# The score products of an HGRN2 scan: four products of 128 columns, or one of 128 and four of 64

## The chip, the cores and the metric

The kernel runs on one core of one Trainium2 chip. The metric is the device time of one launch in microseconds (us). The time before is 2856.59 us, the median of 3 runs that lie between 2854.42 and 2858.09 us. The profile is of one further execution on the same core.

The engines are named as the profile names them: PE (TensorE, the matrix unit; its weight loads have a row of their own, PEld), DVE (VectorE), ACT (ScalarE), POOL (GpSimd) and SP (which only issues DMAs here). L550 means line 550 of the kernel. A "product" is below one call of the matrix multiply in the kernel's source; in float32 each such call becomes two load-and-multiply pairs on PE.

## What is computed

One layer of a hybrid trunk on 2048 latent tokens of width 1024 with a prefix of 256 context tokens: RMS norm, a bidirectional HGRN2 recurrence with 8 heads of width 128, a gated readout, and a convolutional FFN of width 2816. What matters here is the recurrence in its chunkwise form, for one head and one direction:

```python
b = jnp.cumsum(logf, axis=3)                 # decay since the chunk's start
qe = q * jnp.exp(b - b_ref)
ke = k * jnp.exp(b_ref - b)
scores = jnp.einsum('bhnik,bhnjk->bhnij', qe, ke)
scores = jnp.where(mask, scores, 0.0)        # causal
o_intra = jnp.einsum('bhnij,bhnjv->bhniv', scores, v)
```

Backward in time the same is done with the order of tokens reversed, and the outputs of the two directions are added. The reference point `b_ref` of a pair of tokens may be any point as long as both factors stay in range; the result does not depend on it.

## The kernel before

**Stages.** The first 80 us load inputs and make the modulation rows. From there to about 1330 us runs the scan (`mixer_scan`), then a second pass of the scan with the readout, the output projection and the FFN. Only the scan is touched.

**Loops of the scan.** The 18 tiles of 128 tokens (2 of context, 16 of latents) form 6 units of 3 tiles, in two groups of three units (`GROUPS`). For each group, each of 8 heads and each unit of the group, `unit` is called: 48 calls, 3 tiles each. Of the 144 tiles, 16 are context tiles, which get no scores; 128 get them. A tile is split into 4 segments of 32 tokens; a unit has 12 (`NS`).

**One unit.** PE multiplies the normalized input with the head's weights (L356 to L358, three products in a reduced float32 for each part, into `z`), and ACT and DVE turn them into forget gates `F`, values `v`, the gate `st` and queries `q`. DVE scans `F` to running products `S` inside each segment (L448, L461). Then come, for both directions and all 12 segments at once, `ke` (keys, L453 and L454), `rt` (the reciprocal of a segment's whole decay, L463) and `qp` (queries with the decay up to a segment's edge, L467 and L468). POOL makes small tables of segment decays (`TB`, `TX`), and the helper `scaled` (its DVE instruction is L492) multiplies segments by them: `kd`, `qe`, `qi`, `qm`, `km`. In `qe` each query is multiplied by the reciprocal decay of its own segment. ACT copies half of the segments of `ke` to `kx` (L517, L518).

**Scores of a tile** (`part_a`). PE transposes `kd` (L542) and makes four products of 128 by 128 into one PSUM tile `sc`:

- `ke` with `qe` of direction 0 (L550; backward in time) and of direction 1 (L551; forward), of which only the four diagonal blocks of 32 by 32 are used;
- `kx` with a mix of `qp` of both directions (L556), of which the blocks between the two segments of a 64-token pair are used;
- `km` with `qm` (L557), of which the blocks between the two pairs are used.

ACT copies the two quarters of the last to `af` (L561, L562); DVE puts the others there and in `ab` under masks (`copy_predicated`, L563 with `mx`, L564 with `mb`, L565 with `mf`) and adds the two to `at` (L566). In `part_b` PE multiplies `kt` and `v` (L574, the update of the state), `qi` and the state `Sf` (L589) and `at` and `v` (L590); DVE updates `Sf` (L593).

**Order.** The `part_a` and `part_b` calls of a unit are not run in that unit. They are handed on as a list `todo`, and the next unit runs them between its own products (`fill`), in the order part_a 0, part_a 1, part_b 0, part_a 2, part_b 1, part_b 2. So the operands of a score product are made about a unit ahead of it, save in the last unit. On each engine the instructions stand in the order in which they were emitted, with small shifts that the framework makes. Tiles such as `ke`, `qp`, `qe`, `kx` have two buffers, which two units take in turn.

Of the kernel before, what the change touches and what calls it, by code (L numbers as in the profile page):

```python
# [9 lines left out]
F32 = mybir.dt.float32  # L10
F32R = mybir.dt.float32r
BF16 = mybir.dt.bfloat16
U32 = mybir.dt.uint32
AF = mybir.ActivationFunctionType
OP = mybir.AluOpType
# [29 lines left out]
NS = 12  # L45
# [3 lines left out]
def body(ctx, tc, a, out):  # L49
    nc = tc.nc  # L50
    pe, act, dve, pool, sp = nc.tensor, nc.scalar, nc.vector, nc.gpsimd, nc.sync
# [38 lines left out]
    def pool_(stack, name, bufs=1, **kw):  # L90
        return stack.enter_context(tc.tile_pool(name=name, bufs=bufs, reuse_waits="tile", **kw))
# [94 lines left out]
    with ExitStack() as c0:  # L186
# [15 lines left out]
        first = [t for u in GROUPS[0] for t in u]  # L202
        for k in range(KT):
            for i in range(2):
# [3 lines left out]
                for n in range(2):  # L208
                    pe.matmul(mps[2 * i + n], silv[:, k, :], wt[:, n * 512:(n + 1) * 512],
                              start=k == 0, stop=k == KT - 1)  # L210
# [16 lines left out]
        for g in range(2):  # L227
            ks = slice(g * 4, g * 4 + 4)
            for j, hm in enumerate(hms):
                m = 0 if first[j] >= 0 else 1  # L230
# [9 lines left out]
        mx = p0.tile([128, 16], F32, name="mx")  # L240
# [38 lines left out]
    def mixer_scan():  # L279
        gp = pool_(c1, "gp", side="right")  # L280
        xp = pool_(c1, "xp", side="right")
        ps = pool_(c1, "ps", space=PSUM)
# [3 lines left out]
        def in_block(m, blk):  # L286
            n = 128 // blk
            pool.affine_select(out=m, in_=m, pattern=[[-blk, n], [0, blk]],
                               compare_op=OP.is_ge, fill=0.0, base=0, channel_multiplier=1)
            pool.affine_select(out=m, in_=m, pattern=[[blk, n], [0, blk]],  # L290
                               compare_op=OP.is_ge, fill=0.0, base=blk - 1, channel_multiplier=-1)

        def mask(name):
            m = fix.tile([128, 4, 32], F32, name=name)
            pool.memset(m, 1.0)
            return m

        mf, mb, mx = mask("mf"), mask("mb"), mask("mx")
        in_block(mb, 32)
        in_block(mx.rearrange("p (a c) b -> p a (c b)", c=2), 64)  # L300
        dve.tensor_tensor(mx, mx, mb, OP.subtract)
        in_block(mf, 32)
        for m, s in ((mf, 1), (mb, -1)):

            pool.affine_select(out=m, in_=m, pattern=[[32 * s, 4], [s, 32]],
                               compare_op=OP.is_ge, fill=0.0, base=0, channel_multiplier=-s)
        mfu, mbu, mxu = [m.rearrange("p a b -> p (a b)").bitcast(U32) for m in (mf, mb, mx)]
        d1 = fix.tile([128, NS, SEG], BF16, name="d1")
        pool.memset(d1, 0.0)
        pool.memset(d1[:, :, 0:1], 1.0)  # L310
# [51 lines left out]
        def unit(h, w, u, tiles, todo, fine=False):  # L362
# [5 lines left out]
            g0 = 4 * s0  # L368
            lat = slice(g0, NS)
# [82 lines left out]
            ke = gp.tile([128, 2, NS, 32], F32, name="ke", tag="ke", bufs=2)  # L452
# [9 lines left out]
            rt = gp.tile([128, 2, NS], F32, name="rt", tag="rt", bufs=2)  # L462
            dve.reciprocal(rt[:, :, lat], S[:, :, lat, 32])  # L463

            qp = gp.tile([128, 2, NS, 32], F32, name="qp", tag="qp", bufs=2)
# [23 lines left out]
            def scaled(dst, src, w):  # L489

                w = w[..., None].to_broadcast(list(w.shape) + [32])
                dve.tensor_tensor(dst, src, w, OP.mult)  # L492
# [7 lines left out]
            scaled(kd, ke, TBf[:, 0:4:3])  # L500


            qe = gp.tile([128, 2, NS, 32], F32, name="qe", tag="qe", bufs=2)
            scaled(qe[:, :, lat], qp[:, :, lat], rt[:, :, lat])
            qi = gp.tile([128, 2, NS, 32], F32, name="qi", tag="qi", bufs=2)
            scaled(qi[:, :, lat], qp[:, :, lat], TBf[:, 1:3, lat])

# [1 line left out]
            qm = gp.tile([128, NSC, 4, 32], F32, name="qm", tag="qm", bufs=2)  # L509
            km = gp.tile([128, NSC, 4, 32], F32, name="km", tag="km", bufs=2)  # L510
# [2 lines left out]
            scaled(km[:, s0:, 0:2], seg(ke[:, 1])[:, :, 0:2], TX[:, 1, s0:, 0:2])  # L513
            scaled(km[:, s0:, 2:4], seg(ke[:, 0])[:, :, 2:4], TX[:, 1, s0:, 2:4])

            kx = gp.tile([128, NS, 32], F32, name="kx", tag="kx", bufs=2)
            act.activation(kx[:, g0::2], ke[:, 1, g0::2], AF.Copy)  # L517
            act.activation(kx[:, g0 + 1::2], ke[:, 0, g0 + 1::2], AF.Copy)  # L518

            if s0:  # L520
                z = ps.tile([128, s0, 128], F32, name="z", tag="pj", bufs=3)
# [16 lines left out]
            def part_a(s):  # L538
                g4 = slice(4 * s, 4 * s + 4)
                tr = ps.tile([128, 2, 128], F32, name="tr", tag="tr")  # L540
                for d in range(2):
                    pe.transpose(tr[:, d], kd[:, d, g4], ident)  # L542
                kt = gp.tile([128, 2, 128], F32, name="kt", tag="kt", bufs=3)
                act.activation(kt, tr, AF.Copy)
                kts[s] = kt
                if s < s0:
                    return

                sc = ps.tile([128, 4, 128], F32, name="sc", tag="sc", bufs=2)
                pe.matmul(sc[:, 0], ke[:, 0, g4], qe[:, 0, g4], start=True, stop=True)  # L550
                pe.matmul(sc[:, 1], ke[:, 1, g4], qe[:, 1, g4], start=True, stop=True)  # L551

                c0 = qp[:, 0, 4 * s]
                qx = bass.AP(tensor=c0.tensor, offset=c0.offset,
                             ap=[list(c0.ap[0]), [64, 2], [(NS + 1) * 32, 2], [1, 32]])
                pe.matmul(sc[:, 2], kx[:, g4], qx, start=True, stop=True)  # L556
                pe.matmul(sc[:, 3], km[:, s], qm[:, s], start=True, stop=True)  # L557
                at = gp.tile([128, 128], F32, name="at", tag="at", bufs=2)
                af, ab = ABs[count["A"] % 2]
                count["A"] += 1  # L560
                act.activation(af[0:64, 64:128], sc[0:64, 3, 64:128], AF.Copy)  # L561
                act.activation(af[64:128, 0:64], sc[64:128, 3, 0:64], AF.Copy)  # L562
                dve.copy_predicated(af, mxu, sc[:, 2])  # L563
                dve.copy_predicated(af, mbu, sc[:, 0])  # L564
                dve.copy_predicated(ab, mfu, sc[:, 1])  # L565
                dve.tensor_tensor(at, af, ab, OP.add)  # L566
                ats[s] = at

            def part_b(s):
# [33 lines left out]
                sp.dma_start(stash[t][:, 0, h, 1], qi[:, 0, g4].rearrange("p g t -> p (g t)"))  # L603

            order = ((part_a, 0), (part_a, 1), (part_b, 0), (part_a, 2), (part_b, 1), (part_b, 2))
            return [lambda f=f, s=s: f(s) for f, s in order]

# [47 lines left out]
        for g, units in enumerate(GROUPS):  # L655
            for h in range(NH):
                if g == h == 0:
                    w = head0
                else:
                    w = load_feat(h)  # L660
                    load_vg(h, w)
                for u, tiles in enumerate(units):
                    todo, fine = list(unit(h, w, u, tiles, todo, fine)), False
                    if h > 0 and steps < 16 * (g + 1):
                        next(rest, None)
                        steps += 1
                    if g == h == u == 0:
                        todo, fine = with_h(todo, [m[-2:] for m in third], [None] * 3), True
                        todo = [m[0] for m in third[1:]] + todo
                    if g == 0 and h == NH - 2 and u == 2:  # L670
                        todo += [m[0] for m in new[0:2]]
                    if g == 0 and h == NH - 1:
                        loads = [m[0] for m in new[3 * u + 2:3 * u + 5]]
                        todo = with_h(todo, [m[1:] for m in new[3 * u:3 * u + 3]],
                                      loads + [None] * (3 - len(loads)))
                        fine = True
                    if g == 1 and h == NH - 1:
                        if u == 0:
                            todo.append(gate1)
                        for j, k in enumerate(range(3 * u, min(3 * u + 3, KT))):  # L680
                            todo.insert(len(todo) if u < 2 else j,
                                        lambda k=k: out_weight(k))
        for f in todo:
            f()

    mixer_scan()
    c1.close()

# [63 lines left out]
    qp = pool_(fq, "qp", side="right")  # L752
# [70 lines left out]
    first = [Pair(1, q) for q in range(2)]  # L823
# [225 lines left out]
    ps = pool_(fp, "psa", 2, space=PSUM)  # L1049
# [200 lines left out]
    ps = pool_(fb, "psb", 8, space=PSUM)  # L1250
# [169 lines left out]
    for s in range(N):  # L1420
        ph, c = divmod(s, NC)
# [84 lines left out]
```

## Time and profile before

| what | us |
|---|---|
| median of 3 runs | 2856.59 |
| span of the profiled execution, first to last instruction | 2852.8 |
| median less span | 3.8 |
| PE busy in the span | 2803.9 |
| DVE busy in the span | 2080.8 |
| ACT busy in the span | 1176.5 |

The page gives the profiled execution by its span; the 3.8 us between it and the median of the runs lie ahead of the first and behind the last instruction, so the profiled execution's own time is taken as that median. Busy time of an engine is the union of its instructions; PE's instructions are pipelined and overlap, so the start of one to the start of the next, not its duration, is what it costs. The timeline gives starts in us from the start of the span and joins neighbours of one group ("x2": two instructions, the duration from the first one's start to the last one's end). The view of one tile gives shortest, median and longest duration in ns, and the first and last start in us.

### The profile page before, as it was taken

The numbers are of one execution on the slowest core, as the hardware profiler recorded it, in microseconds if no ns is written. First come the engines' busy times: TensorE is split into PE (matmuls) and PEld (weight loads), VectorE is DVE, ScalarE is ACT, GpSimd is POOL, SyncE is SP. The second block draws the span as 40 slices with busy tenths as digits, with TensorE's granted clock in tenths as the row PEclk, the third lists the DMA queues.
The fourth block names the chain that finished last, engine by engine and source line by source line (L and its number), as shares of the span: only waits on it lengthen the run. The fifth ranks groups of instructions, "written<-read, shape, count | busy, mean of one in ns | idle before, by whom it ended". The sixth has DMA issues, their size and how long they took to land. (4 is left out here: it accounts for less than half of the span.)

```text
span 2852.8 us, 43739 instructions
## 1 busy us (share of the span) xinstructions
PE 2803.9 (98%) x16016; PEld 2503.4 (88%) x16016; DVE 2080.8 (73%) x3698; ACT 1176.5 (41%) x2517; POOL 570.1 (20%) x1020
## 2 busy tenths in 40 slices
PE   7999999999999999998999899999999999999999
PEld 4999999999999999998888688888888888887887
DVE  5766666677667566587898787777887777676887
ACT  5433333355333323333555444444444444333343
POOL 2111111121111111111111243433443342000001
PEclk9999999999999999999999999999999999999999
DMA  6222222222232222135778622225522223987663
GB/s 237 67 79 79 84 76 84 79 78 89 85 90 66 80 78 85 61 98 185 266 293 315 227 86 71 88 82 190 187 89 89 76 73 115 310 301 252 194 200 122
DMA packets 202623, 385.51 MB, mean 135 GB/s; under 512 B 26660, under 2 KB 117796, under 8 KB 197160
## 3 DMA queue, kind: packets, MB, share of 16 engines
q1 hardware_dynamic: 199672, 374.46, 39.1%
q10 hardware_dynamic: 2736, 8.26, 0.8%
q8 instruction: 126, 2.06, 0.3%
q14 instruction: 89, 0.73, 0.1%
HBM read 280.65 MB, written 101.99 MB: 134 GB/s over the span
## 5 line engine op out<-in xcount | busy, mean ns | idle before, releaser
L356 PE MATMUL z<-vh,hh 128*128 128x256 f32 (+1 forms) x1024 | 300.3, 293 | 0.0
L358 PE MATMUL z<-vh,hl 128*128 128x256 f32 (+1 forms) x1024 | 293.4, 287 | 0.0
L357 PE MATMUL z<-vl,hh 128*128 128x256 f32 (+1 forms) x1024 | 293.3, 286 | 0.0
L356 PE MATMUL z<-hh,wh 128*128 128x384 f32 x768 | 264.1, 344 | 0.7 <-ACT hh L80 0.7
L357 PE MATMUL z<-hl,wh 128*128 128x384 f32 x768 | 258.4, 336 | 0.5 <-DVE hl L81 0.5
L358 PE MATMUL z<-hh,wl 128*128 128x384 f32 x768 | 258.7, 337 | 0.0
L1338 PE MATMUL y<-wd,ml 128*128 128x512 f32 x600 | 234.0, 390 | 2.1 <-DVE ml L81 2.1
L1336 PE MATMUL y<-wd,mh 128*128 128x512 f32 x600 | 233.8, 390 | 0.9 <-DVE P L1390 0.7
L1337 PE MATMUL y<-wd,mh 128*128 128x512 f32 x600 | 233.5, 389 | 0.0
L356 PEld LDWEIGHTS z<-vh,hh 128*128 128x128 f32 x1024 | 196.3, 192 | 0.0
L357 PEld LDWEIGHTS z<-vl,hh 128*128 128x128 f32 x1024 | 196.1, 191 | 0.0
L358 PEld LDWEIGHTS z<-vh,hl 128*128 128x128 f32 x1024 | 195.8, 191 | 0.0
L81 DVE TENSOR_TENSOR w<-raw,w 128x512 fp32r<-128x512 f32 x180 | 141.9, 793 | 43.1 <-ACT w L80 41.1
L484 POOL COPY TX<-S 128x3 f32<-128x3 f32 x48 | 14.6, 304 | 792.4 <-DVE S L448 792.4
L80 ACT ACTIVATE w<-raw 128x512 fp32r<-128x512 f32 x180 | 111.8, 629 | 141.2 <-PE zd L741 78.6
L81 DVE TENSOR_TENSOR w<-s,w 128x512 fp32r<-128x512 f32 x126 | 122.3, 976 | 49.4 <-ACT w L80 48.6
L424 DVE TENSOR_TENSOR st<-z,st 128x128 f32<-128x128 f32 x127 | 36.5, 287 | 158.7 <-ACT st L423 158.6
L356 PEld LDWEIGHTS z<-hh,wh 128*128 128x128 f32 x768 | 145.3, 189 | 4.4 <-DVE acc L620 1.7
L419 ACT ACTIVATE v<-z 128x128 f32<-128x128 f32 x128 | 35.4, 277 | 271.1 <-PE z L358 271.1
L357 PEld LDWEIGHTS z<-hl,wh 128*128 128x128 f32 x768 | 145.2, 189 | 0.7 <-DVE hl L81 0.7
L358 PEld LDWEIGHTS z<-hh,wl 128*128 128x128 f32 x768 | 144.7, 188 | 0.0
L738 PE MATMUL zc<-rT,w 128*128 128x512 f32 x352 | 137.1, 389 | 2.7 <-ACT w L80 2.7
(337 smaller groups left out, 8119.8 us busy)
## 6 DMA issues: line engine op xcount, KB each, us to landing
raw<-in_w_up_dram SPq DMA_DIRECT2D x88, 512.0 KB, 3.8
raw<-in_w_in_dram SPq DMA_DIRECT2D x80, 512.0 KB, 3.7
lr<-m SPq DMA_DIRECT2D x49, 512.0 KB, 5.5
m<-r SPq DMA_DIRECT2D x66, 256.0 KB, 4.3
raw<-in_w_ada_dram SPq DMA_DIRECT2D x32, 512.0 KB, 4.5
stash<-st SPq DMA_DIRECT2D x125, 128.0 KB, 1.9
kq<-stash SPq DMA_DIRECT2D x15, 1024.0 KB, 7.4
og<-stash SPq DMA_DIRECT2D x15, 1024.0 KB, 6.3
```

What stands on the lines that cost most here:

```text
L80: act.activation(h, src, AF.Copy)
L81: dve.tensor_tensor(l, src, h.bitcast(F32), OP.subtract)
L356: pe.matmul(o, sh[:, k], mh[:, k], start=k == 0, stop=False)
L357: pe.matmul(o, sh[:, k], ml[:, k], start=False, stop=False)
L358: pe.matmul(o, sl[:, k], mh[:, k], start=False, stop=k == KT - 1)
L419: act.activation(v[:, s], z[:, 0:128], AF.Copy)
L424: dve.tensor_tensor(st[:, 1], z[:, 128:256], st[:, 1], OP.mult)
L484: pool.tensor_copy(TX[:, 0, :, 0], tot[:, 0, :, 1])
L738: pe.matmul(o, w[:, 0, k], r[:, :, 0, k], start=start and k == 0, stop=False, skip_group_check=True)
L1336: pe.matmul(z, lh, rh, start=start, stop=False, skip_group_check=True)
L1337: pe.matmul(z, lh, rl, start=False, stop=False, skip_group_check=True)
L1338: pe.matmul(z, ll, rh, start=False, stop=stop, skip_group_check=True)
```

## The change

The scores inside a 64-token pair of segments get one scaling for both kinds of block, the diagonal ones and the one between the two segments. Every column of queries meets one set of keys only, and the reciprocal decay `rt` of a segment is applied either to its query or to its key:

- `qe` goes. In its place two DVE multiplications of half the segments each: `qp` is scaled in place in the odd segments of direction 0 and the even ones of direction 1, and `ke` in the even segments of direction 0 and the odd ones of direction 1 is written, scaled, to `kx`.
- `kx` has two directions in place of one; ACT still copies the same two halves of `ke` into it.
- Per tile, two products with 64 columns for each direction (`ke` with the segments of one parity, `kx` with those of the other) write interleaved 32-column blocks of a direction's score tile. With the `km` product, which now comes first, there are five products in place of four.
- The masks `mb` and `mf` cover a whole causal 64-block; `mx` and its `copy_predicated` go.

```diff
-        mf, mb, mx = mask("mf"), mask("mb"), mask("mx")
-        in_block(mb, 32)
-        in_block(mx.rearrange("p (a c) b -> p a (c b)", c=2), 64)
-        dve.tensor_tensor(mx, mx, mb, OP.subtract)
-        in_block(mf, 32)
+        mf, mb = mask("mf"), mask("mb")
+        for m in (mf, mb):
+            in_block(m.rearrange("p (a c) b -> p a (c b)", c=2), 64)
...
-            qe = gp.tile([128, 2, NS, 32], F32, name="qe", tag="qe", bufs=2)
-            scaled(qe[:, :, lat], qp[:, :, lat], rt[:, :, lat])
...
-            kx = gp.tile([128, NS, 32], F32, name="kx", tag="kx", bufs=2)
-            act.activation(kx[:, g0::2], ke[:, 1, g0::2], AF.Copy)
-            act.activation(kx[:, g0 + 1::2], ke[:, 0, g0 + 1::2], AF.Copy)
+            def halves(x, first):
+
+                c = x[:, 0, g0 + first]
+                step, inner = (32, [1, 32]) if len(x.shape) > 3 else (1, [0, 32])
+                return bass.AP(tensor=c.tensor, offset=c.offset,
+                               ap=[list(c.ap[0]), [(NS + 1 - 2 * first) * step, 2],
+                                   [2 * step, (NS - g0) // 2], inner])
+
+            kx = gp.tile([128, 2, NS, 32], F32, name="kx", tag="kx", bufs=2)
+            act.activation(kx[:, 1, g0::2], ke[:, 1, g0::2], AF.Copy)
+            act.activation(kx[:, 0, g0 + 1::2], ke[:, 0, g0 + 1::2], AF.Copy)
+            dve.tensor_tensor(halves(qp, 1), halves(qp, 1), halves(rt, 1), OP.mult)
+            dve.tensor_tensor(halves(kx, 0), halves(ke, 0), halves(rt, 0), OP.mult)
...
-                sc = ps.tile([128, 4, 128], F32, name="sc", tag="sc", bufs=2)
-                pe.matmul(sc[:, 0], ke[:, 0, g4], qe[:, 0, g4], start=True, stop=True)
-                pe.matmul(sc[:, 1], ke[:, 1, g4], qe[:, 1, g4], start=True, stop=True)
-
-                c0 = qp[:, 0, 4 * s]
-                qx = bass.AP(tensor=c0.tensor, offset=c0.offset,
-                             ap=[list(c0.ap[0]), [64, 2], [(NS + 1) * 32, 2], [1, 32]])
-                pe.matmul(sc[:, 2], kx[:, g4], qx, start=True, stop=True)
-                pe.matmul(sc[:, 3], km[:, s], qm[:, s], start=True, stop=True)
+                sc = ps.tile([128, 3, 128], F32, name="sc", tag="sc", bufs=2)
+                pe.matmul(sc[:, 2], km[:, s], qm[:, s], start=True, stop=True)
+                scv = sc.rearrange("p n (g t) -> p n g t", g=4)
+                for d in range(2):
+                    for i, k in enumerate((ke, kx)):
+                        q0 = (d + 1 + i) % 2
+                        pe.matmul(scv[:, d, q0::2], k[:, d, g4],
+                                  qp[:, d, 4 * s + q0:4 * s + 4:2], start=True, stop=True,
+                                  skip_group_check=True)
...
-                act.activation(af[0:64, 64:128], sc[0:64, 3, 64:128], AF.Copy)
-                act.activation(af[64:128, 0:64], sc[64:128, 3, 0:64], AF.Copy)
-                dve.copy_predicated(af, mxu, sc[:, 2])
+                act.activation(af[0:64, 64:128], sc[0:64, 2, 64:128], AF.Copy)
+                act.activation(af[64:128, 0:64], sc[64:128, 2, 0:64], AF.Copy)
                 dve.copy_predicated(af, mbu, sc[:, 0])
                 dve.copy_predicated(ab, mfu, sc[:, 1])
```

More of the change, by code (lines that the diff above doesn't have):

```diff
@@ L306, in mixer_scan @@
                                compare_op=OP.is_ge, fill=0.0, base=0, channel_multiplier=-s)
-        mfu, mbu, mxu = [m.rearrange("p a b -> p (a b)").bitcast(U32) for m in (mf, mb, mx)]
+        mfu, mbu = [m.rearrange("p a b -> p (a b)").bitcast(U32) for m in (mf, mb)]
         d1 = fix.tile([128, NS, SEG], BF16, name="d1")
```

## The prediction, made before the changed kernel ran

> **What bounds the kernel now.** First the head of the page, for the span and the engine that is always busy; then the busy time by stage, to see whether that holds where the change lies.
>
> ```profile
> span 2852.8 us, 43739 instructions
> PE 2803.9 (98%) x16016; PEld 2503.4 (88%) x16016; DVE 2080.8 (73%) x3698; ACT 1176.5 (41%) x2517; POOL 570.1 (20%) x1020
> ...
> PE   7999999999999999998999899999999999999999
> ```
>
> ```profile
> core 0: us, PE busy (x) PEld busy (x) DVE busy (x) ACT busy (x) POOL busy (x), PEclk, DMA share, GB/s
> ...
> 80.00:1310.00 1230.00, 1225.03 (x8791) 1209.52 (x8790) 826.86 (x1857) 452.48 (x1345) 188.66 (x571) 1.00 0.26 81
> 1310.00:1330.00 20.00, 17.38 (x142) 16.38 (x140) 13.46 (x37) 8.19 (x27) 0.46 (x2) 1.00 0.60 202
> ```
>
> From 80 to 1310 us, where nearly all scores are made, PE idles 1230.00 - 1225.03 = 5.0 us, at the full clock (1.00). DVE is busy 67% of it. So in this stage the time is the sum of PE's steps, and a saving on DVE can return at most those 5.0 us. What counts is how far apart PE's instructions start. The timeline of PE over one tile's products:
>
> ```profile
> 702.62 0.38 PE L542 MATMUL tr<-ident,kd 128*128 128x128 f32 x2
> 702.83 0.39 PE L550 MATMUL sc<-qe,ke 128*128 128x128 f32 x2
> 703.06 0.39 PE L551 MATMUL sc<-qe,ke 128*128 128x128 f32 x2
> 703.28 0.39 PE L556 MATMUL sc<-qp,kx 128*128 128x128 f32 x2
> 703.50 0.39 PE L557 MATMUL sc<-qm,km 128*128 128x128 f32 x2
> 703.73 0.61 PE L574 MATMUL kv<-v,kt 128*128 128x128 f32 x4
> 704.17 0.39 PE L589 MATMUL o<-Sf,qi 128*128 128x128 f32 x2
> 704.40 0.39 PE L590 MATMUL o<-v,at 128*128 128x128 f32 x2
> ```
>
> Every written float32 product is two instructions, each with its weight load. From L550 to L590 lie seven products (L574 is two): (704.40 - 702.83) / 7 = 0.224 us a product, 0.112 us an instruction. Durations of 0.275 us overlap and say nothing here.
>
> **What sets the 0.112 us?** This decides the sign. An instruction of 128 columns has two candidates: streaming its columns, or loading the next 128x128 weights. The change halves the columns and leaves the weights. Streaming alone is seen in the first stage, where the weights have two columns; loading alone in transposes of 2x2, where the columns are two:
>
> ```profile
> 29.74 5.31 PE L209 MATMUL mps<-wada,sil 128*2 128x512 f32 x12
> 34.98 0.90 PE L220 MATMUL mt<-ident,m 2*128 2x2 f32 x12
> ```
>
> ```profile
> L209 PE MATMUL mps<-wada,sil x64: 592/592/1057, 4.9 to 34.5; 128*2 128x512 f32 x64
> ```
>
> ```profile
> L220 PEld LDWEIGHTS mt<-ident,m x16: 133/136/138, 35.0 to 36.7; 2*128 2x128 f32 x16
> L220 PE MATMUL mt<-ident,m x16: 195/196/218, 35.0 to 36.7; 2*128 2x2 f32 x16
> ```
>
> L209: (5.31 - 0.59) / 11 = 0.429 us for 512 columns, 0.84 ns a column; 128 columns stream in 0.107 us and 64 in 0.054. L220: (0.90 - 0.196) / 11 = 0.064 us a step although two columns stream in 2 ns. Something on the weight side, or the issue, costs that. The loads of the scores are longer still; the views of `sc` and of the transposes `tr`:
>
> ```profile
> L550 PEld LDWEIGHTS sc<-qe,ke x256: 186/190/192, 86.4 to 1323.3; 128*128 128x128 f32 x128
> L550 PE MATMUL sc<-qe,ke x256: 271/275/377, 86.5 to 1323.4; 128*128 128x128 f32 x128
> ```
>
> ```profile
> L542 PEld LDWEIGHTS tr<-ident,kd x288: 137/141/145, 74.4 to 1322.5; 128*128 128x128 f32 x144
> L542 PE MATMUL tr<-ident,kd x288: 270/272/331, 74.6 to 1322.6; 128*128 128x128 f32 x144
> ```
>
> A score load takes 190 ns, a transpose's 141. The longest instruction of each line is one that began after an idle and had to wait for its own weights: 377 - 275 = 102 ns for a score, 331 - 272 = 59 ns for a transpose. So from the start of a float32 load to the first column that can use it pass some 102 ns. That hides only if the load starts early enough. Two views of the FFN's product, weight loads and then products, show how early:
>
> ```profile
> 2542.09 0.19 PEld L1336 LDWEIGHTS y<-wd,mh 128*128 128x128 f32 x1 [0.65 <-ACT X L1371]
> 2542.20 0.19 PEld L1337 LDWEIGHTS y<-wd,mh 128*128 128x128 f32 x1
> 2542.43 0.19 PEld L1338 LDWEIGHTS y<-wd,ml 128*128 128x128 f32 x1
> 2542.66 0.19 PEld L1336 LDWEIGHTS y<-wd,mh 128*128 128x128 f32 x1
> ```
>
> ```profile
> 2542.09 0.50 PE L1336 MATMUL y<-wd,mh 128*128 128x512 f32 x1 [0.23 <-ACT X L1371]
> 2542.43 0.39 PE L1337 MATMUL y<-wd,mh 128*128 128x512 f32 x1
> 2542.66 0.40 PE L1338 MATMUL y<-wd,ml 128*128 128x512 f32 x1
> ```
>
> The first product waits for its weights (0.50 against 0.39), until 2542.20, and at 2542.20 the second load starts. The third load, L1338's, starts at 2542.43, exactly with L1337's product, although the load unit had been free since 2542.39. So one load runs ahead and no more: the load of instruction n+1 starts when instruction n begins to stream. However short instruction n is, n+1 streams 102 ns or more after it. With 128 columns (0.107 us of streaming) both limits nearly coincide, so 0.112 us tells them apart no further; with 64 columns the load remains.
>
> **The sum on PE.** Before: 4 products, 8 x 0.112 = 0.896 us a tile. After: `km` with `qm` as before, 2 x 0.112, and four products of 64 columns, 8 instructions. All have 128x128 weights of their own (`ke` and `kx` of two directions), none of which PE holds already. At 0.112 each, 10 x 0.112 = 1.120 us: 0.224 us more for each of the 128 tiles with scores, **+28.7 us**.
>
> The step of a 64-column instruction is not in the trace. Lower bound 102 ns, the wait for the weights: 8 x 0.102 + 0.224 = 1.040, +0.144 us a tile, +18.4 us. Upper bound: the load-bound step of L220, 64 ns, plus the 49 ns by which a score's load is longer, 0.113, and 2 ns for rounding: 0.115, +0.248 us a tile, +31.7 us. I take 0.112, the neighbours' own step. The strided output blocks and strided queries are not shown together, but L556 already reads queries in two runs at L557's step, and any extra has some 50 ns of cover under the load; without the cover it would add to the 0.054, not to the load.
>
> The Trainium skill, page "TensorE: Matmul & The Clock Gate", section "LDWEIGHTS (loading the stationary operand)", prices a load by the weights' columns alone, P/1.2 ns. By it, as an estimate, the step would be 107 ns, 8 x 0.107 + 0.224 = 1.080, and the change +23.6 us; it lies between the bounds.
>
> **The other engines.** DVE and ACT rows that the edit touches, from the tiles' views:
>
> ```profile
> L563 DVE COPY_PREDICATED AB<-mx,sc x128: 273/294/304, 92.5 to 1325.4; 128x128 f32<-128x128 uint32 x128
> L492 DVE TENSOR_TENSOR qe<-qp,rt x48: 414/948/953, 72.6 to 1312.2; 128x768 f32<-128x768 f32 x40, 128x256 f32<-128x256 f32 x8
> L467 DVE TENSOR_TENSOR qp<-q,F x48: 281/549/553, 72.1 to 1311.0; 128x384 f32<-128x384 f32 x40, 128x128 f32<-128x128 f32 x8
> L492 DVE TENSOR_TENSOR qi<-qp,TB x48: 414/948/953, 72.9 to 1313.1; 128x768 f32<-128x768 f32 x40, 128x256 f32<-128x256 f32 x8
> L517 ACT ACTIVATE kx<-ke x48: 256/363/367, 65.1 to 1306.6; 128x192 f32<-128x192 f32 x40, 128x64 f32<-128x64 f32 x8
> ```
>
> ```profile
> PE kv L574 <- DVE Sf L593: 2.9, 5, 0.7
> ```
>
> L563 goes: 128 x 0.294 = 37.6 us of DVE. `qe` goes, 40 x 0.948 + 8 x 0.414 = 41.2 us, and two multiplications of half its size come, priced by L467: 2 x (40 x 0.549 + 8 x 0.281) = 48.4 us. DVE gains 30 us and PE nothing of it, beyond part of its idle; PE's named wait for DVE is 2.9 us. I take 0 and keep 5 us for the range. ACT's copies stay. Three setup instructions on POOL and one on DVE go before the first scores; no wait of PE names them, so 0.
>
> One wait may be added: DVE's write to half of `kx` after ACT's copies to the other half. In the last unit the copy starts at 1306.6 and takes 0.36 us, while the DVE place, beside `qi`, is at 1313.1: six us of cover. Without it, at most 48 x 0.36 = 17 us on DVE, with the `Sf` updates behind it and L574 waiting for those.
>
> Sum: 28.7 us. The span of 2852.8 becomes 2881.5; the median is 3.8 us above the span and I carry that over: 2856.6 + 28.7 = **2885 us**.
>
> **Rivals.** *Faster: the columns decide.* If loads overlap further, the 64-column step is 0.054 us: 8 x 0.054 + 0.224 = 0.656, 0.240 less a tile, -30.7 us, 2826; if L220's 0.064 is the floor, -20.5 us, 2836. The break-even is 8s + 0.224 = 0.896: s = 84 ns. For it: 0.112 is also near 0.107 of streaming. Against: loads start no earlier than the product before them, and L220's step is far above its columns. Chance 0.10.
>
> [...]
>
> *Between.* A step of 75 to 100 ns, with loads partly hidden: 2842 to 2873, break-even inside. No row gives one. Chance 0.05, spread over the signs as 0.01 faster, 0.02 same, 0.02 slower.
>
> *Load-bound, DVE relief returned.* PE gets back all 5.0 us of idle: 2880. Part of the forecast's own range.
>
> *The wait on `kx` bites.* +17 us on DVE; with DVE at 67% it shows on PE only if `Sf` is late: up to 2902. Chance 0.03.
>
> **Chances and range.** Load-bound 0.82, faster rival 0.10, between 0.05, late `kx` 0.03. A measurement here tells about 0.2% (5.7 us) from no change. Faster by over that 0.11, same 0.02, slower 0.87. The forecast's bounds are 2875 and 2888, less up to 5 us of idle returned and plus a few us of shifted order: 2870 to 2892, which leaves out the faster rival, most of the middle and the late `kx`.
>
> **What would show it.** After: five products in a tile, ten starts about 0.112 us apart from `km` to the last; score instructions of 64 columns with loads still near 190 ns; PE busy up by some 29 us between 80 and 1340 us, DVE down by some 30. Wrong if the 64-column starts lie under 84 ns apart.

## The result, and the profile after

The changed kernel takes 2881.86 us, the median of 4 runs (2880.77 to 2884.47), against 2856.23 us for the kernel before in the same comparison: 25.6 us more, ratio 1.009 with a 95% interval of 1.0076 to 1.0105, that is 22 to 30 us. The forecast was 2885 us, 28.7 us more than the median it started from.

The head of the page of after, against that of before:

```profile
span 2880.6 us, 44205 instructions
...
PE 2831.3 (98%) x16272; PEld 2533.0 (88%) x16272; DVE 2078.8 (72%) x3617; ACT 1179.2 (41%) x2517; POOL 586.6 (20%) x1017
```

PE has 256 more load-and-multiply pairs (16272 against 16016; two more in each of 128 tiles) and 27.4 us more busy time; the span grew by 27.8 us. In every run whose span is on record the time is only 1.6 to 2.0 us above the span (after: 2882.31 against 2880.6). So the 3.8 us between before's span and its median are not all time outside the instructions: by the same difference the profiled execution of before took some 2854.6 us, an estimate, 2 us under the median, and the spans differ by 2 us more than the medians. The busy time of the scan, by stage:

```profile
80.00:1340.00 1260.00, 1256.09 (x9102) 1242.59 (x9101) 817.06 (x1787) 455.56 (x1348) 204.85 (x572) 1.00 0.25 79
```

PE idles 3.9 us here, as it idled 5.0 before: the stage is still the sum of PE's steps, at the full clock. The timeline of one tile's products in after, PE first and then its weight loads (two instructions in most rows):

```profile
312.19 0.39 PE L556 MATMUL sc<-qm,km 128*128 128x128 f32 x2
312.42 0.33 PE L561 MATMUL sc<-qp,ke 128*128 128x64 f32 x2
312.59 0.39 PE L561 MATMUL sc<-qp,kx 128*128 128x64 f32 x2
312.81 0.39 PE L561 MATMUL sc<-qp,ke 128*128 128x64 f32 x2
313.03 0.39 PE L561 MATMUL sc<-qp,kx 128*128 128x64 f32 x2
313.26 0.66 PE L579 MATMUL kv<-v,kt 128*128 128x128 f32 x4
```

```profile
312.31 0.30 PEld L561 LDWEIGHTS sc<-qp,ke 128*128 128x128 f32 x2
312.53 0.30 PEld L561 LDWEIGHTS sc<-qp,kx 128*128 128x128 f32 x2
312.75 0.30 PEld L561 LDWEIGHTS sc<-qp,ke 128*128 128x128 f32 x2
312.98 0.30 PEld L561 LDWEIGHTS sc<-qp,kx 128*128 128x128 f32 x2
313.20 0.53 PEld L579 LDWEIGHTS kv<-v,kt 128*128 128x128 f32 x4
```

Look at the load row first: from 312.31 to 313.20 eight loads, 0.89 / 8 = 0.111 us each, back to back, for products of half the columns. Products with 64 columns cost what those with 128 cost. The PE row has one step that looks short: the first `ke` product starts at 312.42 and the next at 312.59, 0.17 us for two. The first short instruction had its weights loaded behind the last long one, streams for 0.054 us and is gone; the next is then recorded as started, and waits for its load. The view of `sc` shows that wait as duration:

```profile
L561 PEld LDWEIGHTS sc<-qp,ke x512: 190/192/193, 85.7 to 1345.7; 128*128 128x128 f32 x171
L561 PE MATMUL sc<-qp,ke x512: 221/275/276, 85.8 to 1345.8; 128*128 128x64 f32 x171
```

221 ns without a wait, 275 ns with one of 54 ns; most have one. The last wait of a tile falls on the product behind it (`kv`, 0.66 us for four against 0.61 before). So the whole tile pays two more loads, although one start in ten comes early.

### The profile page after: what moved, and what is told of

It reads as the page before. It is cut to its first block, busy times and chain, and to the rows that moved or that the text cites. A ratio compares the mean times of both kernels' runs of the same rounds, so it can differ in the third digit from the quotient of the medians.

```text
span 2880.6 us, 44205 instructions
## 1 busy us (share of the span) xinstructions
PE 2831.3 (98%) x16272; PEld 2533.0 (88%) x16272; DVE 2078.8 (72%) x3617; ACT 1179.2 (41%) x2517; POOL 586.6 (20%) x1017
## 4 chain that ended last, share of the span: by engine, by line
PE 88%; DMA 5%; DVE 4%; issue 1%; ACT 1%; POOL 1%; SPq 0%; DVEq 0%; POOLq 0%; ACTq 0%
PE z L354 11%; PE z L356 11%; PE z L355 11%; PE sc L561 4%; PE y L1343 3%; PE y L1341 3%; PE y L1342 3%; PE zd L743 3%; PE zd L746 3%; PE zd L745 3%; PE zc L743 3%; PE zc L745 3%; PE zc L746 3%; PE za L746 3%; PE za L745 3%; PE za L743 3%
## 5 line engine op out<-in xcount | busy, mean ns | idle before, releaser
L482 POOL COPY TX<-S 128x3 f32<-128x3 f32 x48 | 28.3, 589 | 808.5 <-DVE S L446 808.5
L81 DVE TENSOR_TENSOR w<-raw,w 128x512 fp32r<-128x512 f32 x180 | 140.7, 786 | 47.7 <-ACT w L80 45.7
L81 DVE TENSOR_TENSOR w<-s,w 128x512 fp32r<-128x512 f32 x126 | 127.6, 1017 | 41.9 <-ACT w L80 41.4
```

Of the source, the lines that this page charges most:

```text
L81: dve.tensor_tensor(l, src, h.bitcast(F32), OP.subtract)
```

## The experiments

The theory: a float32 product's instruction takes as long as the load of its weights, some 112 ns for 128 weight columns, whatever it streams below that. The rivals: the streamed columns set the step; a fixed cost per instruction does, with the weights' size of no account; the strided output blocks cost the time; DVE's new work or the new order of the products does. Four kernels ran against 17 runs of before (median 2859.31 us), three against 10 (2857.61 us).

**One product for each direction, 128 columns (`one_per_dir`).** `kx` of a direction holds raw keys in one segment of a pair and scaled ones in the other, and it serves the queries of both; `ke` was needed only because masked entries (a scaled query times a scaled key) can leave float32's range (that is the argument for the scaling; no run without it shows such an overflow). Scaling all queries by 2^-64 and the outputs by 2^64 makes room for them.

```diff
-                    for i, k in enumerate((ke, kx)):
-                        q0 = (d + 1 + i) % 2
-                        pe.matmul(scv[:, d, q0::2], k[:, d, g4],
-                                  qp[:, d, 4 * s + q0:4 * s + 4:2], start=True, stop=True,
-                                  skip_group_check=True)
+                    pe.matmul(sc[:, d], kx[:, d, g4], qp[:, d, g4], start=True, stop=True)
...
-            dve.tensor_tensor(qp[:, 0, lat], qv, F[:, 0, lat, 1:SEG], OP.mult)
+            dve.scalar_tensor_tensor(qp[:, 0, lat], qv, 2.0 ** -64, F[:, 0, lat, 1:SEG], OP.mult, OP.mult)
...
-                act.activation(st[:, 0], o, AF.Copy)
+                act.activation(st[:, 0], o, AF.Copy, scale=2.0 ** 64)
...
-                dve.tensor_tensor(o, o, oi, OP.add)
+                dve.scalar_tensor_tensor(o, oi, 2.0 ** 64, o, OP.mult, OP.add)
```

> Three score products of 128 columns per tile: kx with qp for each direction, km with qm. Queries are scaled by 2^-64 and the outputs by 2^64, so that the masked blocks stay finite. Weight loads set the step (theory): 6 instructions of 0.112 us in place of 8 before and 10 after, 28.7 us under before, 2828 us, with up to 5 us less if DVE's relief counts. Columns set the step (rival): 384 columns as in the changed kernel, so its 2882 us. A fixed cost per instruction (second rival) gives 2828 us too.

Measured: 2831.38 us (4 runs, 2829.01 to 2833.83), ratio to before 0.9905 (0.989 to 0.992), 23 to 31 us less; the load theory's 28.7 lies inside. It streams as many columns in a tile as after (384) and takes 50 us less, so the streamed columns do not set the time. It leaves nothing of the computation out and beats both kernels. Its PE timeline, three products, `sc<-qp,kx` being two of them in one row:

```profile
302.78 0.39 PE L556 MATMUL sc<-qm,km 128*128 128x128 f32 x2
303.01 0.61 PE L558 MATMUL sc<-qp,kx 128*128 128x128 f32 x4
303.45 0.61 PE L574 MATMUL kv<-v,kt 128*128 128x128 f32 x4
```

From 302.78 to 303.45 are 0.67 us for six instructions, 0.112 each.

**The new DVE work with before's count of products (`four_of_128`).**

```diff
+                pe.matmul(sc[:, 2], km[:, s], qm[:, s], start=True, stop=True)
                 pe.matmul(sc[:, 2], km[:, s], qm[:, s], start=True, stop=True)
...
-                    for i, k in enumerate((ke, kx)):
-                        q0 = (d + 1 + i) % 2
-                        pe.matmul(scv[:, d, q0::2], k[:, d, g4],
-                                  qp[:, d, 4 * s + q0:4 * s + 4:2], start=True, stop=True,
-                                  skip_group_check=True)
+                    pe.matmul(sc[:, d], ke[:, d, g4], qp[:, d, g4], start=True, stop=True)
```

> The changed kernel's DVE, ACT and POOL work with before's number of product instructions: km with qm twice and ke with qp for each direction, all of 128 columns. The blocks for which kx was needed come out differently, so it computes other scores. Weight loads set the step (theory): 8 instructions as before, 2856 us, or up to 5 us less from DVE's relief. If the extra time came from DVE's new multiplications or their waits (rival), it stays near 2882 us.

Measured: 2862.11 us (12 runs, 2856.08 to 2864.01), ratio 1.0008 (1.0 to 1.0017). All of DVE's, ACT's and POOL's changes together cost nothing to 5 us, and DVE's relief gives nothing back. The rest of the change's 25.6 us is PE's.

**Half the columns again (`cols_32`).**

```diff
-                        pe.matmul(scv[:, d, q0::2], k[:, d, g4],
-                                  qp[:, d, 4 * s + q0:4 * s + 4:2], start=True, stop=True,
+                        pe.matmul(scv[:, d, q0], k[:, d, g4],
+                                  qp[:, d, 4 * s + q0], start=True, stop=True,
...
-                dve.copy_predicated(af, mbu, sc[:, 0])
+                dve.copy_predicated(af[:, 0:64], mbu[:, 0:64], sc[:, 0, 0:64])
```

> The changed kernel with 32 columns in each of the four short products, written to contiguous blocks; the scores of the queries of the second 64 tokens of a tile inside their pairs are left out. Weight loads or a fixed cost per instruction set the step: 2882 us as after, within 2 us. Columns set the step (rival): 8 x 27 ns less per tile, 27.6 us, 2854 us. Strided output blocks cost the time (rival): 2850 us or less.

Measured: 2883.36 us (4 runs), ratio 1.0086 (1.0073 to 1.0099): after's time. Its PE timeline:

```profile
312.19 0.39 PE L561 MATMUL sc<-qp,kx 128*128 128x32 f32 x2
312.42 0.39 PE L561 MATMUL sc<-qp,ke 128*128 128x32 f32 x2
312.64 0.39 PE L561 MATMUL sc<-qp,kx 128*128 128x32 f32 x2
312.86 0.69 PE L579 MATMUL kv<-v,kt 128*128 128x128 f32 x4
```

0.67 us for six instructions of 32 columns, 0.112 each, written to contiguous blocks. The columns and the strided blocks both fall as causes.

**Narrower weights (`keys_64`, `keys_96`, `keys_32`).** The same four products, with the keys of the first 64, 96 or 32 tokens of a tile as weights; `keys_32` also streams 32 columns. The edit of `keys_64`, the others likewise:

```diff
-                        pe.matmul(scv[:, d, q0::2], k[:, d, g4],
+                        pe.matmul(scv[0:64, d, q0::2], k[:, d, 4 * s:4 * s + 2],
...
-                dve.copy_predicated(af, mbu, sc[:, 0])
+                dve.copy_predicated(af[0:64], mbu[0:64], sc[0:64, 0])
```

> The changed kernel with weights of 64 columns (the keys of the first 64 tokens of a tile) in each of the four short products; the scores of the other keys inside their pairs are left out. Weight loads set the step (theory): half the load, so the 64 streamed columns and the load come to about 58 ns each, 8 x 0.054 us less per tile, 55 us less than after, 2827 us. A fixed cost per instruction (rival): 2882 us as after.

Measured: 2879.76 us (4 runs, 2878.89 to 2880.56), ratio 1.0072 (1.0059 to 1.0085). By its time the theory was refuted and a fixed cost per instruction borne out. The trace says otherwise. PE's timeline, its loads, and the load's row in the view of `sc`:

```profile
310.43 0.39 PE L556 MATMUL sc<-qm,km 128*128 128x128 f32 x2
310.75 0.33 PE L561 MATMUL sc<-qp,ke 128*64 128x64 f32 x2
310.91 0.28 PE L561 MATMUL sc<-qp,kx 128*64 128x64 f32 x2
311.03 0.28 PE L561 MATMUL sc<-qp,ke 128*64 128x64 f32 x2
311.15 0.28 PE L561 MATMUL sc<-qp,kx 128*64 128x64 f32 x2
311.36 0.71 PE L579 MATMUL kv<-v,kt 128*128 128x128 f32 x4
```

```profile
310.32 0.30 PEld L556 LDWEIGHTS sc<-qm,km 128*128 128x128 f32 x2
310.75 0.19 PEld L561 LDWEIGHTS sc<-qp,ke 128*64 128x64 f32 x2
...
311.36 0.52 PEld L579 LDWEIGHTS kv<-v,kt 128*128 128x128 f32 x4
```

```profile
L561 PEld LDWEIGHTS sc<-qp,kx x512: 132/138/138, 85.8 to 1338.9; 128*64 128x64 f32 x171
```

Inside the short products the step did fall, to 0.06 us (310.91, 311.03, 311.15, two instructions each). But the load of the first narrow weights starts at 310.75. The last `km` instruction began near 310.54 (0.11 after 310.43), and streams for 0.107 us, to 310.65; in after the next load starts with that instruction, here 0.10 us after its end. The same happens on the way back: the last short instruction begins near 311.21, and the `kv` load not then but at 311.36, after which `kv` waits another 0.10 us for its weights. So at both changes of the weights' width, twice in a tile, the load isn't taken ahead here, and that returns most of the gain. From the first `km` start to the first `kv` load of the rows above are 0.93 us, against 1.01 in after (312.19 to 313.20): of the 0.43 us a tile that the theory expected, 0.08 stay, 10 us over 128 tiles. In the profiled execution the scan ends earlier than in after by a similar amount, 7.1 us, as the first product of the second pass, `oi`, shows (1341.7 against 1348.8, whose row stands further below):

```profile
L863 PE MATMUL oi<-Sb,kq x256: 270/275/553, 1341.7 to 1545.9; 128*128 128x128 f32 x128
```

The stages behind the scan, whose code is the same, took 5.3 us longer in that execution than in after's, so that the spans, like the medians, differ by only 2 us. Why those stages took longer stays open.

**Weights of 96 columns (`keys_96`).**

> The changed kernel with weights of 96 columns in the four short products; the scores of the keys of the last 32 tokens of a tile inside their pair are left out. A load's time goes by its columns (theory): 0.085 us a step in place of 0.112, 8 x 0.027 us less per tile, 28 us less than after, 2854 us, less whatever a change of width costs (with the 64-column weights about 0.1 us before and after the short products). A load of anything above 64 columns costs as much as 128 (rival): 2882 us.

Measured: 2865.23 us (7 runs, 2863.02 to 2868.26), ratio 1.0029 (1.0017 to 1.0040), 5 to 11 us over before where after is 22 to 30 over. PE's timeline, then the loads' row:

```profile
309.03 0.33 PE L561 MATMUL sc<-qp,kx 128*96 128x64 f32 x2
309.20 0.33 PE L561 MATMUL sc<-qp,ke 128*96 128x64 f32 x2
309.37 0.33 PE L561 MATMUL sc<-qp,kx 128*96 128x64 f32 x2
309.54 0.55 PE L579 MATMUL kv<-v,kt 128*128 128x128 f32 x3
```

```profile
L561 PEld LDWEIGHTS sc<-qp,kx x512: 161/165/165, 85.8 to 1326.1; 128*96 128x96 f32 x171
```

0.51 us for six instructions, 0.085 each, as the theory said, with no gap at the change of width. A fixed cost per instruction falls. The gain against after, about 17 us by the two ratios, is under the 28 expected. Look at where a tile's loads begin and end:

```profile
308.78 0.27 PEld L561 LDWEIGHTS sc<-qp,ke 128*96 128x96 f32 x2
...
309.48 0.30 PEld L579 LDWEIGHTS kv<-v,kt 128*128 128x128 f32 x2
```

The eight take 0.70 us here and 0.89 in after. That is 0.19 us less, seven times 0.027 and not eight: the first step still lasts 0.11 (0.27 for two loads, less one of 0.165), since the last `km` instruction streams its 128 columns in it. Seven give 24 us; the other 7 us are within the two intervals.

**Weights of 32 columns (`keys_32`).**

> The changed kernel with weights of 32 columns and 32 streamed columns in the four short products; most scores inside the pairs are left out. If only load and stream count (theory): steps of about 0.031 us between short products. If an instruction has a floor of its own (rival): 0.06 us, as with the 2x2 transposes and the 64-column weights. In both, idle of about 0.1 us where the width of the weights changes.

Measured: 2846.41 us (one run). PE's timeline and the loads' row:

```profile
305.14 0.23 PE L561 MATMUL sc<-qp,kx 128*32 128x32 f32 x2
305.20 0.23 PE L561 MATMUL sc<-qp,ke 128*32 128x32 f32 x2
305.26 0.23 PE L561 MATMUL sc<-qp,kx 128*32 128x32 f32 x2
305.42 0.71 PE L579 MATMUL kv<-v,kt 128*128 128x128 f32 x4
```

```profile
L561 PEld LDWEIGHTS sc<-qp,kx x512: 106/113/114, 85.1 to 1307.9; 128*32 128x32 f32 x171
```

0.12 us for four instructions, 0.030 each: no floor of 0.06. Put together:

| weight columns | streamed columns | load, median ns | step, ns | kernel |
|---|---|---|---|---|
| 128 | 128 | 190 to 192 | 112 | before |
| 128 | 64 | 192 | 112 | after |
| 128 | 32 | 192 | 112 | cols_32 |
| 96 | 64 | 165 | 85 | keys_96 |
| 64 | 64 | 136 to 138 | 60 | keys_64 |
| 32 | 32 | 110 to 113 | 30 | keys_32 |

The load's duration and the step go down together, by 25 to 30 ns for each 32 weight columns. The streamed columns change neither at 128 weight columns, the only width at which they were varied alone. With 64 weight columns a load by this slope (some 55 ns) and the streaming of 64 columns (54 ns) cost about the same, so that row does not tell them apart, and `keys_32` narrowed both.

The Trainium skill, page "TensorE: Matmul & The Clock Gate", section "LDWEIGHTS (loading the stationary operand)", gives P/1.2 ns for P weight columns; the slope here, 27 ns for 32 columns, agrees with it, and the steps lie 3 to 7 ns above it.

**The order of the products (`km_last`).** The changed kernel with the `km` product behind the others:

```diff
-                pe.matmul(sc[:, 2], km[:, s], qm[:, s], start=True, stop=True)
                 scv = sc.rearrange("p n (g t) -> p n g t", g=4)
...
                                   skip_group_check=True)
+                pe.matmul(sc[:, 2], km[:, s], qm[:, s], start=True, stop=True)
```

> The changed kernel with the km product behind the four short ones, as before had it. Weight loads set the step and the order does not matter (theory): 2882 us, within 2 us. If the order took part in the change (rival), it moves by more than 5 us.

Measured: 2884.15 us (4 runs), ratio 1.0091 (1.0076 to 1.0106), as after. The order takes no part.

## Why the prediction was right

**The bound.** The reading that the scan is the sum of PE's steps held: PE idles 3.9 us of 1260 in after, and `four_of_128` shows that nothing off PE moved the time by more than 5 us.

**What sets the 0.112 us.** The choice of the load over the columns is shown, from both sides: columns halved twice at equal weights change nothing (after, `cols_32`), and weights narrowed at equal columns shorten the step (`keys_96`). Fewer weight columns also give fewer output rows; what ties the step to the load is that the load's own row shrinks with it (165 ns against 192, step 85 against 112). The rows that carried it were the wait of a product behind an idle (102 ns) and the start of each load with the product before it. The third row, L220's step of 64 ns, was offered as "the weight side, or the issue"; `keys_32` shows that the issue allows 30.

**The sum.** 0.224 us a tile was forecast, and after's loads give it: eight in 0.89 us, two more than before in each of 128 tiles, 28.7 us. `one_per_dir`, with two fewer instructions, gives -28 us by its medians. The span grew by 27.8, the median by 25.6 with an interval that includes 28.7. Where the profiled executions put it can be read from the first product of the second pass, `oi`, in before, after, `one_per_dir` and `four_of_128`:

```profile
L858 PE MATMUL oi<-Sb,kq x256: 270/275/347, 1327.1 to 1528.5; 128*128 128x128 f32 x128
```

```profile
L863 PE MATMUL oi<-Sb,kq x256: 270/275/552, 1348.8 to 1550.3; 128*128 128x128 f32 x128
```

```profile
L858 PE MATMUL oi<-Sb,kq x256: 270/275/553, 1296.1 to 1497.9; 128*128 128x128 f32 x128
```

```profile
L859 PE MATMUL oi<-Sb,kq x256: 270/275/347, 1324.8 to 1528.1; 128*128 128x128 f32 x128
```

Against `four_of_128`, which has all of the change but PE's part, the scan of `one_per_dir` ends 28.7 us earlier, the size forecast, and that of after 24.0 later. Against before, after's scan ends 21.7 later, and the stages behind it, whose code is the same, take 6 us longer in that execution. A part of the difference in the scan is PE's waits for DVE, which shrank from 2.9 us to:

```profile
PE kv L579 <- DVE Sf L598: 0.9, 2, 0.6
```

A likely reason, not tested, is that with more of PE's time in front of them the state updates are late less often. The remaining few us in the scan, and the 6 behind it, stay open; they are as large as the spread between single executions (before ran from 2853.74 to 2863.76).

**The step of 64 columns** was priced between 102 and 115 ns and taken as 112: the loads come at 111 to 112. One detail was forecast wrongly: that all ten starts would lie 0.112 apart. The first short instruction is left after 0.06 us, since its own load was hidden; the loads, not the starts, keep the even step, and the time is repaid by the next product. Two readings behind the price were off without harm. The upper bound added to L220's step the 49 ns between a score's load and that of L542 (141 ns); L220's own loads take 136, so the difference is 54, and the bound by the same working 120 ns, not 115. And L556 reads its queries in four runs of 32 columns (`qx` in the diff), not two.

**The other engines.** DVE lost `qe` (41.2 us) and L563 (37 us) and got two multiplications, here in their full-size form, 40 of 48 each:

```profile
L524 DVE TENSOR_TENSOR kx<-ke,rt 128x384 f32<-128x384 f32 x40 | 22.2, 555 | 0.0
L523 DVE TENSOR_TENSOR qp<-qp,rt 128x384 f32<-128x384 f32 x40 | 22.1, 553 | 0.9
```

That is the price by L467 (549 ns) that was forecast, and the wait on ACT's copies that could have come before them shows as 0.0 and 0.9 us of idle: the cover was there.

The relief itself was forecast too large, 30 us. From 80 us to the first `oi` product DVE is busy for 822.1 us in after and for 837.5 in before, 15.4 less (18.7 less in `four_of_128`). The forecast added durations, but neighbouring DVE instructions overlap. Two `copy_predicated` of before that follow each other:

```profile
1298.27 0.30 DVE L564 COPY_PREDICATED AB<-mb,sc 128x128 f32<-128x128 uint32 x1
1298.47 0.30 DVE L565 COPY_PREDICATED AB<-mf,sc 128x128 f32<-128x128 uint32 x1
```

They start 0.20 us apart and last 0.30. At 0.20 each, L563 was worth some 25 us and not 37.6. Behind the scan DVE was busy 12.8 us longer in after's execution (FFN's `r<-r`, L1097, 63.0 us against 54.2, and `w<-s,w`, L81, 127.6 against 122.3), so the page's total fell by only 2 us. None of this reaches the forecast of the time, which took DVE's relief as 0.

**The rivals.** The columns' rival, 2826 to 2836, is refuted, and with it the middle one (whose lower end, by its own step of 75 ns, is 2847 and not 2842). The wait on `kx` did not come. DVE's relief returned nothing that the times show.

## What to carry to other kernels

Before cutting the columns of a product, ask what each instruction waits for: here, with 128 weight columns of its own and 128 or fewer float32 columns to stream, it was the load, and a product of 64 columns cost one of 128. Count loads, then, and give each as many columns as it can serve: here one scaling for a pair of segments is worth 28 us when it removes a product, and costs 26 us when it splits the products in more. If an experiment's time comes out as a rival said, look at its steps before giving up the theory; in `keys_64` the gain was there, and a new idle beside it.

## What was not expected of the hardware

- Weights of 64 or 32 columns between weights of 128: the load isn't taken ahead at either change of width, which leaves PE some 0.1 us without a load each time (`keys_64`: 310.65 to 310.75). With 96 columns there is no such gap. Why 64 and 32 lose it and 96 does not is not shown.
- The loads of float32 transposes take 141 ns and those of products with the same 128x128 shape 190 to 192; the difference, about 50 ns, is close to that between 64 and 128 weight columns of a product (138 and 192).
- With 32 weight columns and 32 streamed columns PE starts a float32 instruction every 30 ns (`keys_32`: four between 305.14 and 305.26).
